# Three modulation banks of layer 1: out of the latent scan, into the loops of the first split FFN

## The chip, the core and the metric

The kernel runs on one core of one Trainium2 chip. The core has five engines that run at the same time, each through its own list of instructions and strictly in that list's order: TensorE (PE: matmuls, with its weight loads shown apart as PEld), VectorE (DVE), ScalarE (ACT), GpSimd (POOL) and SyncE (SP). They wait for one another through semaphores. SP, ACT and POOL also issue DMAs, which 16 DMA engines carry out; an issue that has to wait (for a buffer to come free) holds up whatever stands behind it in the same engine's list. The metric is the device time of one execution, in microseconds (us).

## What is computed

Two layers of a trunk over 128 context tokens and 1024 latent tokens, with 1024 features. Cut to what matters:

```python
def ada_mod(cond, w, b):
    m = (jax.nn.silu(cond) @ w + b)[..., None, :]
    return jnp.split(m, 6, axis=-1)

for i in range(DEPTH):                      # DEPTH = 2
    sh1c, sc1c, g1c, sh2c, sc2c, g2c = ada_mod(c_ctx, ada_w[i], ada_b[i])
    sh1l, sc1l, g1l, sh2l, sc2l, g2l = ada_mod(c, ada_w[i], ada_b[i])
    hc = modulate(xc, sh1c, sc1c)
    hl = modulate(xl, sh1l, sc1l)
    # layer 0: oc, ol = s5_mixer(hc), s5_mixer(hl): scan, output, gelu, GLU;  layer 1: pool_mixer
    xc = layer_norm(DEEPNORM_ALPHA * xc + g1c * oc, ln_g[i, 0], ln_b[i, 0])
    xl = layer_norm(DEEPNORM_ALPHA * xl + g1l * ol, ln_g[i, 0], ln_b[i, 0])
    fc = swiglu(modulate(xc, sh2c, sc2c), ffn_w_gate[i], ffn_w_up[i], ffn_w_down[i])
    fl = swiglu(modulate(xl, sh2l, sc2l), ffn_w_gate[i], ffn_w_up[i], ffn_w_down[i])
    xc = layer_norm(DEEPNORM_ALPHA * xc + g2c * fc, ln_g[i, 1], ln_b[i, 1])
    xl = layer_norm(DEEPNORM_ALPHA * xl + g2l * fl, ln_g[i, 1], ln_b[i, 1])
```

The modulation `ada_mod` depends only on the two conditioning vectors and on `ada_w` (1024 x 6144 in each layer), so it can be computed at any time before its first use. The first use of layer 1's modulation lies behind all of layer 0.

## The kernel before

The 1024 latent tokens are two blocks, A and B, of 512 tokens; the 128 context tokens are a third, C. A block lies feature-major: 128 partitions x 8 feature tiles x tokens. The latent GEMMs are *split* (lines 760 to 761 and 776 to 778): ACT writes a weight's high part `wh`, DVE the remainder `wl`, and PE makes three matmuls for each product. The context's GEMMs use the raw weight in one matmul (line 780), which the trace shows as two records. Weights come in blocks of 512 KB, by SP, into a ring of three buffers (`self.raw`, line 769); the splits have rings of three for `wh` and `wl`.

The modulation is cut into five banks of 2048 columns besides the first one: (layer 0: 1, 2; layer 1: 0, 1, 2). A bank is 16 steps of a generator (`ada_steps`, line 131). A step loads 512 KB of `ada_w` by SP (line 146, the tile `adaw`) and makes four matmuls of 32 x 256 on four column groups of the array (line 148), eight records in the trace. The 16th step goes on: ACT copies the sums out (`arow`, line 154), four small DMAs on ACT's queue regroup them (`ar`, line 158), PE transposes them (`adat`, line 160), and DVE adds the bias and derives vectors (line 161 and `vecs`). A caller takes steps with `self.step(fill, n)`, or one behind each item of a loop with `self.drain(loop, fill)`.

The program around the change runs in this order. `ssm` builds the states' inputs with 16 steps in its loops, then the context's mixer outputs (`ssm_y_ctx`) with another 16. Then come `ctx0a` (the context's GLU and LayerNorm), `ssm_scan_lat` (the latents' scan, on DVE) and the 48 steps of the three banks of layer 1; then `ssm_y` for eight feature tiles (matmuls `py`, lines 607 and 611; their gelu goes to DRAM as `yd`). While the pool `ssy` of this part is open, `self.adp` points to it and `adaw` has two buffers of its own there; once it is `None`, steps take their buffers, and `arow`'s, from `self.raw`, and their sums another PSUM tag. Behind `ssm`, `build` runs the context's channel mixing (`ctx0b`: 22 pairs of gate and up weights, then down weights; tile `rc`, from a pool in halves of a block, once the latents have theirs), reads the latents back (`yr`, line 1095, on POOL's queue, two buffers; `xr`, transposed by PE as `px`), then GLU of A and B, LayerNorm, and the split FFN of layer 0: `ffn_up` for A (22 pairs, 48 matmuls each), `ffn_down` for A (22 weights, 24 matmuls each), the same for B.

None of this fixes the order of the instructions alone. A scheduler takes the program's order as priority, simulates the engines, and writes each engine's list; so matmuls of `ctx0b`, the steps and `py` are interleaved on PE, and their loads on SP.

```python
self.ctx0a()
self.ssm_scan_lat()
self.step(fill, 48)
self.adp = self.rawc = None
for kt in range(KT):
    self.ssm_y(tmp, kt)
```

Of the kernel before, what the change touches and what calls it, by code (L numbers as in the profile page):

```python
# [11 lines left out]
F32 = mybir.dt.float32  # L12
# [5 lines left out]
DRAM = bass.MemoryType.DRAM  # L18
# [23 lines left out]
class Kernel:  # L42
# [3 lines left out]
    # ---------------------------------------------------------------- helpers  # L46
# [20 lines left out]
    def cmul(self, eng, pool, o_re, o_im, a, b, shape, tag, nb_im=None, p=None):  # L67
        """o = a * b for complex pairs; with nb_im = -b_im the imaginary part comes out negated."""
# [15 lines left out]
    # ------------------------------------------------------------- constants  # L84
    def consts(self):
# [16 lines left out]
        # mod[l]: [128, vec, cond, kt]; vec = sh1, sc1, g1, sh2, sc2, g2  # L102
# [27 lines left out]
    # --------------------------------------------------------- conditioning  # L130
    def ada_steps(self, l, b, pool=None):
        """Columns 2048*b.. of layer l's modulation, for both conditions, in small steps."""
# [45 lines left out]
    # ------------------------------------------------------------------ SSM  # L178
    def ssm_params(self, pool, tmp, ad):
# [31 lines left out]
        self.h0 = self.sk.tile([128, 2, 2, 32], F32, name="h0")   # dir, re/im, gpair  # L211
# [19 lines left out]
        # powers of the discretized diagonal: [128, re/im, exponent 0..8, (dir, gpair)]  # L231
# [12 lines left out]
        # input coefficient  # L244
# [15 lines left out]
        # scan multipliers per direction: [128, dir, (Rr|Rr|-?), ...]  # L260
        rm = self.sk.tile([128, 2, 2, 2, 32], F32, name="rm")      # dir, term, re/im, gpair
# [7 lines left out]
        # B and C with the states on the partitions: [128, re/im, (dir, gpair), 16]  # L269
# [28 lines left out]
    def ssm_modvec(self, pool, tmp, arow):  # L298
        """(1 + sc1) and sh1 per (token in chunk, channel) partition: [128, cond, (sh, sc), g]."""
# [20 lines left out]
    def ssm_u(self, tmp, kt):  # L320
        """u[(s,h), g, chunk]: the modulated mixer input; also the context's residual."""
# [23 lines left out]
    def ssm_u_ctx(self, tmp):  # L345
# [3 lines left out]
        # partitions are (feature tile, chunk)  # L349
# [25 lines left out]
    def load_x(self):  # L375
        """Feature-major residual of the latents."""
# [13 lines left out]
    def ssm_in(self, tmp, d, kt, tp, nb):  # L390
        """Chunk inputs V of direction d's state recurrence for 8 groups, written into the state slots."""
# [41 lines left out]
    def scan_step(self, *steps):  # L433
        """State slots: dst += A^8 src, for each (direction, src, dst); the steps are independent."""
# [37 lines left out]
    def ssm_dskip(self, pool, tmp):  # L472
        """D on the partitions (group of 8, h'): [128, kt]; selector of h == h'; zeroed B blocks."""
# [12 lines left out]
        # block-diagonal B of group pairs: [128 = (group of 2, state), dir, re/im, pair, (group of 2, h')]  # L486
# [4 lines left out]
    def ssm_tables(self, tmp, kt, si):  # L491
        """Output tables and in-chunk kernels of 8 groups, to DRAM in the layout of the output products."""
# [59 lines left out]
    def ssm_y_ctx(self, tmp, kt):  # L552
        """Mixer output (after gelu) of the context for 8 groups, feature-major."""
# [29 lines left out]
        # the last ones stay on chip: partitions (group pair, chunk); a group's features go to its own columns,  # L583
        # the rest of them stay zero
# [12 lines left out]
    def ssm_y(self, tmp, kt):  # L597
        """Mixer output (after gelu) of the latents for 8 groups, to DRAM feature-major."""
# [23 lines left out]
    def ssm(self):  # L622
# [43 lines left out]
        with R("ssy") as tmp:  # L666
# [11 lines left out]
            self.step(fill, 48)  # L678
# [13 lines left out]
    def ctx0a(self):  # L692
        """The context's mixer output projection of layer 0."""
        C, xmc = self.C, self.xmc
        self.glu(C, [xmc], vx=lambda a: a.rearrange("p (c t) -> p t c", t=8),
                 vs=lambda a: a.rearrange("p (t c) -> p t c", t=8))
        self.ln(C, 0, 0, [xmc])

    def ctx0b(self):
        """The context's channel mixing of layer 0, in steps."""  # L700
# [5 lines left out]
    def ctx1a(self, tmp):  # L706
        """The context's pool mixer."""
# [8 lines left out]
    def ctx1b(self):  # L716
        """The context's channel mixing of layer 1, in steps."""
# [6 lines left out]
    # -------------------------------------------------------- derived vectors  # L724
# [498 lines left out]
```

## Time and profile before

| | before |
|---|---|
| runs (3), median | 2500.75 us |
| lowest, highest | 2499.89, 2501.96 us |
| span of the profiled execution | 2493.0 us |
| median less that span | 7.75 us |
| PE busy in the span | 2296.9 us (92%) |
| DMA moved in the span | 370.63 MB, 149 GB/s |
| steps (`adaw` loads, 512 KB each) | 96, of which 48 are issued from 307.21 us on |

The profiled execution has no device time of its own in the records, only its span. Times below are us from the span's start. "PEclk" is the clock that was granted to TensorE, as a share of the full one; the DMA share is the mean busy share of the 16 DMA engines. A stretch in which PE has gaps and the DMA share is about 1 waits for data; one in which PE is busy throughout is bound by PE.

### The profile page before, as it was taken

How to read it: one execution, taken by the hardware profiler on the slowest of the kernel's cores; microseconds unless marked ns; L12 is line 12 of the kernel's file. 1: busy time of each engine (PE TensorE's matmuls, PEld its weight loads, DVE VectorE, ACT ScalarE, POOL GpSimd, SP SyncE). 2: the span in 40 equal slices, each digit the busy share in tenths (PEclk: the TensorE clock that was granted, in tenths of full speed). 3: DMA queues.
4: the chain of work that ended last, by engine and by line, in shares of the span. 5: the costliest groups of instructions: out<-in, count | busy, mean ns of one | idle time of the engine just before them, and what ended most of it. 6: DMA issues, size and time to landing. Idle time of an engine off the chain costs nothing.

```text
span 2493.0 us, 33897 instructions
## 1 busy us (share of the span) xinstructions
PE 2296.9 (92%) x13533; PEld 1880.8 (75%) x13533; DVE 1252.8 (50%) x2429; ACT 895.0 (36%) x1321; POOL 191.2 (8%) x190
## 2 busy tenths in 40 slices
PE   4685779979999999999999999889999999999997
PEld 2453557668888788888888888777788888888996
DVE  7579771024444632455422585778422455422476
ACT  3673211134423422433422353325322443322464
POOL 4760000000001000100000010002000100000000
PEclk8897889999999999999999999999999999999998
DMA  7767888796454333223333224874333223333352
GB/s 219 218 203 286 278 262 262 219 313 178 142 156 129 101 93 100 95 98 96 94 98 97 99 96 137 236 204 142 94 96 97 95 93 95 92 97 96 136 202 103
DMA packets 465246, 370.63 MB, mean 149 GB/s; under 512 B 19792, under 2 KB 414816, under 8 KB 462784
## 3 DMA queue, kind: packets, MB, share of 16 engines
q1 hardware_dynamic: 445296, 349.29, 45.5%
q10 hardware_dynamic: 18448, 14.58, 1.8%
q0 software_dynamic: 1344, 4.59, 0.5%
q8 instruction: 106, 1.74, 0.3%
q14 instruction: 52, 0.43, 0.1%
HBM read 345.36 MB, written 22.94 MB: 148 GB/s over the span
## 4 chain that ended last, share of the span: by engine, by line
PE 79%; DMA 13%; ACT 3%; DVE 2%; SPq 1%; issue 1%; POOL 1%; ACTq 0%; DVEq 0%; POOLq 0%
PE ffn L778 13%; PE ffn L776 13%; PE ffn L777 13%; PE dn L777 6%; PE dn L776 6%; PE dn L778 6%; PE ffn L780 4%; DMA adaw<-ada_w 3%; PE py L611 3%; PE dn L780 2%; DMA raw<-ffn_w_up 2%; PE glu L777 2%; PE glu L778 2%; PE glu L776 2%; DMA raw<-ffn_w_gate 2%; PE ada L148 1%
## 5 line engine op out<-in xcount | busy, mean ns | idle before, releaser
L760 ACT ACTIVATE wh<-raw 128x1024 fp32r<-128x1024 f32 (+1 forms) x326 | 341.6, 1049 | 944.0 <-PE ffn L777 619.6
L761 DVE TENSOR_TENSOR wl<-raw,wh 128x1024 fp32r<-128x1024 f32 (+1 forms) x326 | 394.6, 1211 | 482.9 <-ACT wh L760 475.5
L777 PE MATMUL dn<-hkl,wh 128*128 128x512 f32 (+1 forms) x880 | 304.3, 348 | 0.3 <-DVE hkl L761 0.3
L778 PE MATMUL dn<-hkh,wl 128*128 128x512 f32 (+1 forms) x880 | 302.9, 347 | 0.0
L776 PE MATMUL ffn<-xp,wh 128*128 128x512 f32 x704 | 280.3, 398 | 2.3 <-ACT wh L760 2.3
L778 PE MATMUL ffn<-xp,wl 128*128 128x512 f32 x704 | 280.5, 398 | 0.5 <-DVE wl L761 0.5
L777 PE MATMUL ffn<-xp,wh 128*128 128x512 f32 x704 | 278.1, 395 | 0.0
L776 PE MATMUL ffn<-xm,wh 128*128 128x512 f32 x704 | 273.3, 390 | 2.8 <-ACT wh L760 2.1
L778 PE MATMUL ffn<-xm,wl 128*128 128x512 f32 x704 | 275.7, 392 | 0.0
L777 PE MATMUL ffn<-xm,wh 128*128 128x512 f32 x704 | 274.9, 390 | 0.2 <-DVE xm L761 0.2
L776 PE MATMUL dn<-hkh,wh 128*128 128x512 f32 (+1 forms) x880 | 259.4, 347 | 0.8 <-ACT hkh L760 0.8
L821 DVE TENSOR_TENSOR h<-ffn,sg 128x512 f32<-128x512 f32 x88 | 60.5, 688 | 254.0 <-PE ffn L778 253.3
L777 PEld LDWEIGHTS dn<-hkl,wh 128*128 128x128 f32 x880 | 166.6, 189 | 21.1 <-DVE hkl L761 0.5
L778 PEld LDWEIGHTS dn<-hkh,wl 128*128 128x128 f32 x880 | 166.5, 189 | 20.5
L776 PEld LDWEIGHTS dn<-hkh,wh 128*128 128x128 f32 x880 | 163.3, 189 | 21.8 <-ACT hkh L760 1.3
L780 PE MATMUL ffn<-xmc,raw 128*128 128x128 f32 x1184 | 150.1, 284 | 23.4 <-DMA raw<-ffn_w_gate 10.6
L780 PEld LDWEIGHTS ffn<-xmc,raw 128*128 128x128 f32 x1184 | 142.3, 197 | 37.7 <-DMA raw<-ffn_w_up 13.9
L776 PEld LDWEIGHTS ffn<-xp,wh 128*128 128x128 f32 x704 | 132.7, 189 | 34.1 <-ACT wh L760 2.5
L777 PEld LDWEIGHTS ffn<-xp,wh 128*128 128x128 f32 x704 | 132.9, 189 | 33.8 <-issue 0.7
L778 PEld LDWEIGHTS ffn<-xp,wl 128*128 128x128 f32 x704 | 132.9, 189 | 33.8 <-DVE wl L761 1.0
L776 PEld LDWEIGHTS ffn<-xm,wh 128*128 128x128 f32 x704 | 132.5, 188 | 32.2 <-ACT wh L760 3.0
L777 PEld LDWEIGHTS ffn<-xm,wh 128*128 128x128 f32 x704 | 132.5, 188 | 28.4 <-DVE xm L761 0.9
(305 smaller groups left out, 3209.5 us busy)
## 6 DMA issues: line engine op xcount, KB each, us to landing
raw<-ffn_w_down SPq DMA_DIRECT2D x126, 512.0 KB
raw<-ffn_w_gate SPq DMA_DIRECT2D x125, 512.0 KB
raw<-ffn_w_up SPq DMA_DIRECT2D x125, 512.0 KB
adaw<-ada_w SPq DMA_DIRECT2D x96, 512.0 KB
raw<-ssm_glu_w SPq DMA_DIRECT2D x48, 512.0 KB
mo<-mo SPq DMA_DIRECT2D x16, 1536.0 KB
rc<-ffn_w_down SPq DMA_DIRECT2D x40, 256.0 KB
mo<-otab SPq DMA_DIRECT2D x16, 512.0 KB
```

Source lines behind the costliest of these rows:

```text
L148: nc.tensor.matmul(ps[32 * cg:32 * cg + 32, 256 * hf:256 * hf + 256], self.cond[:, k, :], w[:, cg * 256:(cg + 1) * 256], start=(k == 0), s ...
L611: nc.tensor.matmul(o[x], ot[64 * x:64 * x + 64, d, r, gp, :], self.Z[d][64 * x:64 * x + 64, d:d + NCL, 32 * r + 4 * kt + gp], start=False, ...
L760: nc.scalar.activation(h, src, AF.Copy)
L761: nc.vector.tensor_tensor(l, src, h.bitcast(F32), op=OP.subtract)
L776: nc.tensor.matmul(ps, wh, xh, start=start, stop=False)
L777: nc.tensor.matmul(ps, wh, xl, start=False, stop=False)
L778: nc.tensor.matmul(ps, wl, xh, start=False, stop=stop)
L780: nc.tensor.matmul(ps, w[0], x[0], start=start, stop=stop)
L821: nc.vector.tensor_tensor(h[:, f, :], pu, sg, op=OP.mult)
```

## The change

The call that takes the 48 steps behind the scan is gone. Nothing is put in its place: the generator is still held as `self.ada`, and the loops of layer 0's split FFN already draw from it (`fill = self.ada`, then `drain` of `ffn_up(A)`, `ffn_down(A)` and `ffn_up(B)`, each with `fill`). Before, it was empty there. Now it gives one step behind each of A's 22 pairs, one behind each of A's 22 down weights, and the last four behind B's first pairs. Since `self.adp` is `None` by then, their loads and `arow` take buffers of `self.raw`.

```diff
             self.ctx0a()
             self.ssm_scan_lat()
-            self.step(fill, 48)
             self.adp = self.rawc = None
             for kt in range(KT):
                 self.ssm_y(tmp, kt)
```

The rest of the diff takes out comments and docstrings. Lines behind 678 have one number less in the changed kernel (780 becomes 779).

PE's list from the context's LayerNorm (`lnm`, `lnv`) to the latents' output products, before (`ffn` is the context's channel mixing, `ada` a step):

```order
L148 MATMUL ada_3997<-adaw_4046,cond 32x256 x4
L780 MATMUL ffn<-xmc,raw 128x128 x8
L148 MATMUL ada_3997<-adaw_4052,cond 32x256 x4
L780 MATMUL ffn<-xmc,raw 128x128 x5
L148 MATMUL ada_3997<-adaw_4058,cond 32x256 x4
L780 MATMUL ffn<-xmc,raw 128x128 x11
L148 MATMUL ada_3997<-adaw_4064,cond 32x256 x4
L148 MATMUL ada_3997<-adaw_4070,cond 32x256 x4
L780 MATMUL ffn<-xmc,raw 128x128 x24
```

and now:

```order
L779 MATMUL glu<-xmc,raw 128x128 x37
L862 MATMUL lnm<-lt,ones 128x128
L862 MATMUL lnv<-sq,ones 128x128
L779 MATMUL ffn<-xmc,raw 128x128 x100
L611 MATMUL py_4000<-Z_648,mo 128x128
...
L779 MATMUL ffn<-xmc,raw 128x128 x44
L611 MATMUL py_4000<-Z_1796,mo 128x128
```

The steps are gone from between the context's matmuls. Eight matmuls are one weight: 144 of them, 18 weights, now stand ahead of the main run of `py`, where 14 weights stood; 12 instead of 16 stand behind it. On SP the `adaw` loads between the weights' loads are gone likewise.

PE's list in `ffn_up` of block A, at the end of the 16th pair (`ffn_7905` is its up product, `ffn_7969` the next gate product), before:

```order
L776 MATMUL ffn_7905<-xm_5092,wh 128x512
L777 MATMUL ffn_7905<-xm_5093,wh 128x512
L778 MATMUL ffn_7905<-xm_5092,wl 128x512
L776 MATMUL ffn_7969<-xm_5092,wh 128x512 [waits Activation_49]
L777 MATMUL ffn_7969<-xm_5093,wh 128x512
```

and now, where the first of the three banks ends (`adaw_7728` is its 16th load, `ffn_7745` and `ffn_7746` the next pair):

```order
L777 MATMUL ffn_7664<-xm_4760,wl 128x512
L148 MATMUL ada_6662<-adaw_7728,cond 32x256 [waits DMAHW0_49]
L148 MATMUL ada_6662<-adaw_7728,cond 32x256 x3
L160 MATMUL adat_7741<-ident,ar_7736 128x32 [waits DMAHW5_49,DMAHW6_49,DMAHW4_49,DMAHW3_49]
L775 MATMUL ffn_7745<-xm_4760,wh 128x512 [waits Activation_49]
L776 MATMUL ffn_7745<-xm_4761,wh 128x512
L775 MATMUL ffn_7746<-xm_4760,wh 128x512 [waits Activation_49]
```

A step stands behind each pair, and the bank's transpose directly behind its 16th step, with no matmul between. The second bank ends in the same way in `ffn_down` of A, the third behind the fourth pair of B.

ACT's list at the same place now (`sg` is the pair's gate, the four DMAs wait for `arow`):

```order
L819 ACTIVATE sg<-ffn_7663 128x512 [waits DVE_49,PE_49]
L154 ACTIVATE arow_7734<-ada_6662 128x512 [waits DMAHW2_49,DVE_49,PE_49]
L158 DMA ar_7736<-arow_7734 8x1x128 [waits Activation_49]
L158 DMA ar_7736<-arow_7734 8x1x128
L158 DMA ar_7736<-arow_7734 8x1x128 [waits DMAHW5_49]
L158 DMA ar_7736<-arow_7734 8x1x128
L759 ACTIVATE wh<-raw 128x1024 [waits DMAHW1_49]
L759 ACTIVATE wh<-raw 128x1024 [waits DMAHW2_49]
```

The copy and its four DMAs stand ahead of the next pair's two splits.

## Rows read from the trace of the kernel before

**Rows 1.** The page: busy tenths of PE and the DMA engines in 40 slices.
```profile
PE   4685779979999999999999999889999999999997
DMA  7767888796454333223333224874333223333352
```

**Rows 2.** Windows: stretch, length, busy of PE, PEld, DVE, ACT, POOL; PEclk, DMA, GB/s.
```profile
298.00:329.00 31.00, 25.34 (x227) 20.89 (x227) 26.50 (x156) 2.80 (x7) 0.00 (x0) 1.00 0.99 299
...
389.00:484.50 95.50, 95.50 (x756) 68.20 (x754) 0.83 (x4) 9.95 (x18) 0.00 (x0) 1.00 0.70 230
484.50:524.00 39.50, 32.84 (x305) 27.27 (x304) 1.75 (x6) 3.67 (x9) 0.00 (x0) 1.00 1.04 304
524.00:564.20 40.20, 29.24 (x195) 23.62 (x196) 14.07 (x20) 21.44 (x32) 3.25 (x6) 0.96 0.98 313
...
600.00:665.50 65.50, 65.50 (x336) 55.90 (x335) 22.46 (x25) 22.53 (x25) 0.00 (x0) 1.00 0.45 130
...
1064.00:1180.00 116.00, 116.00 (x512) 95.67 (x511) 63.20 (x73) 46.23 (x62) 0.00 (x0) 1.00 0.28 91
```

**Rows 3.** The chain that ended last, from 340 to 490: start, length, what.
```profile
343.85 3.71 PE ffn L780 x16
...
386.74 2.05 PE ffn L780 x16
...
404.24 0.64 PE py L607 x4
404.88 1.93 PE py L611 x16
...
421.81 1.48 PE py L611 x10
...
423.86 1.04 PE py L611 x6
...
486.50 0.57 PE ada L148 x8
487.07 1.09 PE ffn L780 x8
```

**Rows 4.** Timeline of SP's queue: start, length, queue, line, operation, tile, count.
```profile
329.98 21.00 SPq L146 DMA_DIRECT2D adaw<-ada_w  x8
```

**Rows 5.** Timeline of POOL, from 330 to 620 (idle before, and its releaser, in brackets).
```profile
340.83 5.72 POOL L914 TENSOR_SCALAR xmc<-XC,lnm 128x128 f32<-128x128 f32 x8 [66.09 <-issue]
536.14 1.13 POOL L1095 DMA_DIRECT2D yr<-yd  x2 [189.59 <-ACT X L387]
```

**Rows 6.** SP's queue in the context FFN of layer 1: first and last of 25 issues.
```profile
1529.27 0.37 SPq L769 DMA_DIRECT2D raw<-ffn_w_up  x1
...
1583.79 0.37 SPq L769 DMA_DIRECT2D raw<-ffn_w_up  x1
```

**Rows 7.** SP's queue behind the latents' outputs.
```profile
520.41 1.85 SPq L146 DMA_DIRECT2D adaw<-ada_w  x2
...
535.64 0.93 SPq L1189 DMA_DIRECT2D rc<-ffn_w_gate  x2
```

**Rows 8.** Timeline at the end of the first bank, where nothing else stands on PE.
```profile
47.47 1.08 PE L148 MATMUL ada<-adaw,cond 128*32 128x256 f32 x8 [0.32 <-DMA adaw<-ada_w]
...
49.24 2.97 ACTq L158 DMA_DIRECT2D ar<-arow  x4
...
53.59 0.28 PE L160 MATMUL adat<-ident,ar 32*128 32x32 f32 x1 [5.04 <-DMA ar<-arow]
```

**Rows 9.** Timeline of PE behind a short idle time in the split FFN.
```profile
816.00 0.50 PE L776 MATMUL ffn<-xm,wh 128*128 128x512 f32 x1 [2.12 <-ACT wh L760]
...
819.64 0.50 PE L776 MATMUL ffn<-xm,wh 128*128 128x512 f32 x1
```

**Rows 10.** The page's groups of the two splits: busy us, mean ns of one, idle before.
```profile
L760 ACT ACTIVATE wh<-raw 128x1024 fp32r<-128x1024 f32 (+1 forms) x326 | 341.6, 1049 | 944.0 <-PE ffn L777 619.6
L761 DVE TENSOR_TENSOR wl<-raw,wh 128x1024 fp32r<-128x1024 f32 (+1 forms) x326 | 394.6, 1211 | 482.9 <-ACT wh L760 475.5
```

## The prediction

> **What bounds the kernel now.** First the page [rows 1]: PE is at nine tenths in most slices, and its low digits lie in the first eight slices, just where the DMA digits are 6 to 9; from about the eleventh slice on PE is full and the DMA engines a third busy. So the kernel has two regimes, data first and PE later, and the change moves 48 steps from the first to the second. Then the windows [rows 2], to see where between 298 us and 665 us which of the two holds. In the context's GLU (298 to 329) the DMA engines are at 0.99 and PE has gaps. While the latents' outputs `py` are made (389 to 484.5) PE is busy for all of 95.50 us and the DMA engines have room (0.70). From 484.5 to 564.2 it is data again: 304 and 313 GB/s, DMA share about 1, PE idle for 17.6 of 79.7 us. From then on PE has the work: the share falls to 0.45 by 600 to 665.5, with PE full, and to 0.28 in the FFN of layer 0 (1064 to 1180), where 512 matmuls take 116.00 us, 0.227 each. The chain [rows 3] gives the prices on PE in these stretches, SP's and POOL's lists [rows 4 to 7] what the loads wait for, and three places outside of them [rows 8 to 10] what a bank's end, a short idle time and a weight's split cost. So a step that goes is worth its DMA time in two stretches and its PE time in a third, and a step that comes costs its PE time in a stretch where PE has none to spare.
>
> **What is gained: the outputs start earlier.** Of the 48 loads, the first of them issued at 307.21, three stand ahead of the last GLU weights; at 0.524 MB and 299 GB/s they are 5.3 us of DMA time. With them gone the ring of three buffers sets the pace: alone it brings 24 weights in 54.5 us, 2.27 us each [rows 6]. I take 4 us of the 5.3. Then the LayerNorm, where PE waits in any case, and the first weight, which POOL's `xmc` paces (5.72 us from 340.83 [rows 5]): it ended at 343.85 + 3.71 = 347.56 [rows 3], with steps standing ahead of it on PE; without them and 4 us earlier it ends soon after the last `xmc`, at about 342. Then 17 weights more, since 18 instead of 14 now stand ahead of `py`: two lie in the ring, one at the lower clock (3.71) and one at the full one (2.05), then 15 x 2.27 = 34.1; together 39.8, so `py` begins at about 382. Before, it began at 386.74 + 2.05 = 388.8, though with four weights less, because SP stood for 21 us with eight step loads ahead of the next weight [rows 4]. Ends: 378.5 if PE (2.05 each) paces, 388.8 if nothing is won.
>
> **The outputs get shorter.** Twenty records of `py` take 0.64 + 1.93 = 2.57 us where nothing cuts in [rows 3]; 640 are 82.2 us, and ten of them (1.5) stand earlier, so 80.8 remain of 95.7. The 18 steps in between took 18 x 0.57 = 10.3; the rest, 4.6, is what a cut costs: the sixteen records of 1.93 us took 1.48 + 1.04 with a step in them. So `py` ends at 382 + 80.8 = 463 instead of 484.5, which is 21.5 us.
>
> **The stretch behind them has less to move.** Before: 39.5 x 304 + 40.2 x 313 = 24.6 MB [rows 2]. Ten step loads fall away (the last two at 520.41 [rows 7]), 5.2 MB, and the four weights that now stand ahead, 2.1 MB. 17.3 MB at 308 GB/s are 56 us. `yr` and the first `rc` loads waited for the pool `ssy`, which the last bank held until 535.64 [rows 5, 7]; now the last `yd` write holds it, a few us behind `py`, and until then only the ring loads (231 GB/s by its 2.27): 2 us more. 58 instead of 79.7, to 521 instead of 564.2. Behind it PE is full as before, so it all counts: **43 us gained**. Ends: 33, if `py` begins where it did (388.8 + 80.8 = 469.6) and the stretch takes 62; 51, if `py` begins at 378.5 and the stretch takes 54.
>
> **What is paid: 48 steps where PE is full.** A step is 0.57 us, and the eight records behind one took 1.09 where half of 2.05 is 1.03 [rows 3]: 0.63, x 48 = 30.4. I take this row and not the cut in `py` (0.6 more), since `py` runs in pairs on half of the rows and the FFN's matmuls use all 128, as these do. The loads are 0.524 MB for every 6 or 11 us in a stretch whose DMA share is 0.28 [rows 2]; they hide there. Ends: 27.4 and 33.
>
> **Three ends of a bank.** PE's list has the transpose directly behind the 16th step, so PE stands through the copy and four DMAs: 5.04 us, and 0.28 for itself [rows 8]; x 3 = 16.0. Before, the three transposes lay behind other work. Queued behind the waiting one are all of the FFN's matmuls; behind the four issues (2.97 us of ACT's queue) stand the next two splits, 1.05 each with 1.21 on DVE [rows 10]. Counted from the step, the first `wl` comes at about 0.6 + 3 + 1.05 + 1.2 = 5.9 and the second `wh` at 5.8, where PE asks at 5.3 to 6: nothing to a further 1 us each; I take nothing and keep 3 for the range.
>
> **The clock behind each.** After 2.12 us of idle time PE needed 3.64 us for nine starts [rows 9], which the full clock gives in 9 x 0.227 = 2.04 [rows 2]: 1.6 lost; x 3 = 4.8. After the longer idle time ahead of 343.85 one weight lost 1.66 [rows 3], so 2.5 each is the upper end.
>
> The sum of the costs is 30.4 + 16.0 + 4.8 = **51 us**, between 46 (steps at 0.57, two of them in the gaps of B's LayerNorm, the clock half as dear) and 60 (33, 19, 7.5).
>
> Net 51 - 43 = +8. On the profiled span, 2493.0 + 8 = 2501; the runs' median is 7.75 above that span, so **2509 us**.
>
> **The rivals.** *The gain is smaller.* The ring alone might not keep its pace beside `mo` and `xr`, and `py` begin at 388.8; then 33 are gained, +18, 2519 us. For it: the loads of the GLU took longer than 2.27 with the DMA engines full. Against it: no step load stands between them any more.
>
> *Faster: the ends of the banks don't stall and the gain is full.* If the four DMAs of `ar` land while PE still works off queued matmuls, only the steps are paid, 30.4, and at a gain of 43 it comes out at -13: 2488 us. It decides at the place of the transpose: four or five matmuls, 5.3 us of them, between the 16th step and the transpose would do. Against it: the list has none.
>
> *Faster by regimes.* If every step load had lengthened a stretch bound by data, 48 x 0.524 = 25.2 MB at 308 GB/s, 82 us, would be gained, and 51 - 82 = -31: 2470 us. Against it: 18 of the steps ran beside `py`, where PE and not data was the bound [rows 2], and eight in the LayerNorm. The Trainium skill, in "Perfetto Trace Analysis" (Optimization Strategy), says that a kernel whose most contended engine changes over time may gain by interleaving its regimes, which is this change's shape; by that rule alone one would expect this rival's sign. The windows agree that there are two regimes, but the rule leaves out that a step brings PE work with its bytes.
>
> *Slower still: the FFN's ring starves.* A step's load takes a buffer out of three in `self.raw`. In `ffn_down` a step and a weight alternate every 24 x 0.227 + 0.6 = 6.0 us. If the down weights have one buffer, each must land and be split before the next is asked for: by the ring's cycle of 3 x 2.27 less one weight on PE (2.05), 4.8, plus 1.05 + 1.21 = 7.0. Then each of 22 weights loses up to 1.0, and +8 becomes +30: 2531 us. It decides where landing takes more than 3.7 us. Against it: these loads have a third of the DMA's share beside them, and the splits run ahead by up to three.
>
> *Nothing to be measured.* Gain and cost are both near 50 and cancel within 5 us: 2496 to 2506. About 0.2%, 5 us, is what a measurement of this kernel can tell from no change.
>
> **How the numbers follow.** The forecast (+2 to +16) has 0.50, and about a third of that lies within 5 us; the smaller gain 0.20; the ends without a stall 0.11; regimes 0.04; the starving ring 0.06; the exact cancelling 0.09. Faster: 0.11 + 0.04 = 0.15. Within 0.2%: 0.16 + 0.09 = 0.25. Slower: the rest, 0.60. The range leaves out both faster rivals' times and the starving ring's, some 0.2: from 2495 (cost 46, gain 51, so -5 or 2496, and 1 us of scatter) to 2524 (cost 58 with a gain of 35).
>
> **What would show it.** Right, step by step: the main run of `py` begins near 382 and holds no `ada`; it ends near 463; a stretch of some 58 us at 300 GB/s follows, and the first down product of the context (665.5 before) comes some 43 us earlier. Then 48 groups `ada` of about 0.57 us in A's FFN and the first pairs of B; three idle times of about 5 us on PE released by the DMA `ar`, each with a lower PEclk for some us behind it. PE's waits for `wh` or for `raw` weights there should not grow. Wrong: `py` that begins at 388 (smaller gain); no 5 us of idle time at the transposes (faster); waits of PE for `wh` at each down weight (the ring); a first down product later than 640.

## The result and the profile of the changed kernel

The changed kernel took 2522.0 us (median of 4 runs, 2520.2 to 2526.8) against 2500.3 for the kernel before on the same chip; the ratio is 1.0099, 95% interval [1.0083, 1.0114]. It is slower by 21.7 us. The forecast was 2509, so +8: the sign was right and the time lies inside the range, near its upper end, but of the 21.7 us of loss it had only 8. The two profiled executions differ by 2518.4 - 2493.0 = 25.4 us, and the working below is made on those. (The changed kernel's profiled run took 2520.19, 1.8 us over its span; of the kernel before, the run of 2494.85 fits its span in the same way. The "7.75" of the prediction set the median against the span of what was probably the fastest run, which shifts both kernels and not the difference.)

| us from the span's start | before | changed | difference | foreseen |
|---|---|---|---|---|
| first context FFN matmul | 343.85 | 344.29 | +0.4 | about -4 |
| `xmc` starts (POOL, end of the context's LayerNorm) | 340.83 | 342.44 | +1.6 | -4 |
| last step of the scan on DVE ends | 383.35 | 387.81 | +4.5 | not named |
| main run of `py` starts | 388.7 | 390.8 | +2.1 | 382 |
| `py` ends | 484.5 | 469.7 | -14.8 | 463 |
| first split FFN product of block A | 793.89 | 760.79 | -33.1 | -43 |
| sums of block B's second LayerNorm start | 1431.63 | 1456.82 | +25.2 | +8 |
| end | 2493.0 | 2518.4 | +25.4 | +8 |

So the part in front gained 33 instead of 43, and the split FFN paid 58 instead of 51: +25. The windows of the changed kernel, by stretch (length, busy time and count of PE, PEld, DVE, ACT and POOL, granted clock, DMA share, GB/s), answer to [rows 2]:

```profile
298.00:331.00 33.00, 27.06 (x231) 23.39 (x229) 27.54 (x163) 3.14 (x8) 0.00 (x0) 1.00 0.84 252
331.00:344.30 13.30, 1.24 (x5) 0.81 (x5) 13.24 (x63) 3.26 (x8) 1.86 (x2) 0.67 0.18 50
344.30:391.00 46.70, 40.80 (x310) 38.10 (x312) 32.43 (x176) 7.51 (x18) 4.06 (x7) 0.95 0.65 185
391.00:469.70 78.70, 78.70 (x611) 63.15 (x610) 0.29 (x1) 9.14 (x17) 0.00 (x0) 1.00 0.52 159
469.70:531.00 61.30, 45.03 (x354) 41.65 (x354) 19.91 (x26) 30.27 (x46) 4.29 (x8) 0.97 0.98 301
```

The loads did leave: the GLU's stretch falls to a DMA share of 0.84, the LayerNorm's to 0.18 and that of `py` to 0.52. In the LayerNorm's 13.3 us nothing takes the steps' place: PE is busy for 1.24 us of them while DVE is busy throughout. Behind `py` stand 61.3 us at 301 GB/s, 18.4 MB; that stretch is as full of data as before and only shorter.

In the split FFN two places tell where the time is paid. First PE at an ordinary step (start, length, line, tiles; the length of one matmul overlaps the next, so the distance of starts is what counts):

```profile
823.07 0.39 PE L777 MATMUL ffn<-xm,wl 128*128 128x512 f32 x1
823.39 0.64 PE L148 MATMUL ada<-adaw,cond 128*32 128x256 f32 x8
823.96 0.50 PE L775 MATMUL ffn<-xm,wh 128*128 128x512 f32 x1
824.30 0.39 PE L776 MATMUL ffn<-xm,wh 128*128 128x512 f32 x1
...
835.07 0.64 PE L148 MATMUL ada<-adaw,cond 128*32 128x256 f32 x8
```

From one step to the next are 835.07 - 823.39 = 11.68 us; the 48 products between them need 48 x 0.2266 = 10.88. A step costs 0.80: 0.57 from its start to the next product's, 0.09 because the product ahead gives it 0.32 instead of 0.227, and 0.11 because the first product behind gives the second 0.34.

Then PE's waits between 760 and 1450 (what waited for what, total, times, longest), and the place of the first bank's end on PE (with the window behind it), ACT, DVE and SP (idle time before an instruction, and its releaser, in brackets), which answers to [rows 8]:

```profile
PE adat L160 <- DMA ar<-arow: 13.0, 3, 4.5
PE ffn L777 <- DVE wl L760: 1.5, 1, 1.5
PE ffn L775 <- ACT xm L759: 0.7, 1, 0.7
```

```profile
951.87 0.64 PE L148 MATMUL ada<-adaw,cond 128*32 128x256 f32 x8
956.96 0.28 PE L160 MATMUL adat<-ident,ar 32*128 32x32 f32 x1 [4.45 <-DMA ar<-arow]
957.17 0.80 PE L775 MATMUL ffn<-xm,wh 128*128 128x512 f32 x1
957.77 0.63 PE L776 MATMUL ffn<-xm,wh 128*128 128x512 f32 x1
958.20 0.63 PE L775 MATMUL ffn<-xm,wh 128*128 128x512 f32 x1
```

```profile
957.17:959.50 2.33, 2.33 (x7) 1.84 (x7) 1.98 (x4) 0.67 (x2) 0.00 (x0) 0.50 0.53 160
```

```profile
952.58 0.60 ACT L154 ACTIVATE arow<-ada 128x512 f32<-128x512 f32 x1 [5.44 <-PE ada L148]
953.21 2.27 ACTq L158 DMA_DIRECT2D ar<-arow  x4
955.52 2.00 ACT L759 ACTIVATE wh<-raw 128x1024 fp32r<-128x1024 f32 x2 [2.35 <-DMA ar<-arow]
```

```profile
956.61 1.23 DVE L760 TENSOR_TENSOR wl<-raw,wh 128x1024 fp32r<-128x1024 f32 x1 [3.87 <-ACT wh L759]
```

```profile
940.89 0.37 SPq L768 DMA_DIRECT2D raw<-ffn_w_gate  x1
952.57 0.37 SPq L768 DMA_DIRECT2D raw<-ffn_w_up  x1
956.96 0.34 SPq L146 DMA_DIRECT2D adaw<-ada_w  x1
957.86 0.37 SPq L768 DMA_DIRECT2D raw<-ffn_w_gate  x1
```

PE stands for 4.45 us, then works at the lower clock for five starts (0.43 apart instead of 0.227; the granted clock of that window is 0.50). To the next step, at 969.70, are 17.83 us instead of 11.68: 6.15 for one bank's end, taken three times below (the third costs 6.25, the second, where a piece of another step follows the transpose, about 5.6). The ACT rows show the copy and its DMAs ahead of the next two splits, and the SP rows show the up weight of the next pair issued at 952.57, directly behind the 16th step: until then a step's load had held its buffer. (An ordinary pair has its up weight issued 11.6 us ahead of its first product, 824.09 for 835.64; here it is 4.6 us.) Two bounds end here nearly together: the transpose starts at 956.96, and the first split of the next pair, held behind `arow` and its DMAs though its weight was issued at 940.89, is done at about 956.6, when DVE goes on from it. So by these rows moving the transpose alone would win back some 0.4 us. What `arow`'s place in the ring has to do with it is what two experiments below are for.

### The profile page after: what moved, and what is told of

It reads as the page before. It is cut to its first block, busy times and chain, and to the rows that moved or that the text cites. A ratio compares the mean times of both kernels' runs of the same rounds, so it can differ in the third digit from the quotient of the medians.

```text
span 2518.4 us, 33876 instructions
## 1 busy us (share of the span) xinstructions
PE 2308.6 (92%) x13533; PEld 1880.2 (75%) x13533; DVE 1252.2 (50%) x2429; ACT 894.5 (36%) x1321; POOL 185.3 (7%) x190
## 4 chain that ended last, share of the span: by engine, by line
PE 78%; DMA 10%; issue 4%; DVE 3%; ACT 2%; POOL 1%; SPq 1%; ACTq 0%; POOLq 0%; DVEq 0%
PE ffn L775 13%; PE ffn L777 13%; PE ffn L776 13%; PE dn L775 6%; PE dn L776 6%; PE dn L777 6%; PE ffn L779 3%; PE py L611 2%; PE dn L779 2%; PE glu L777 2%; PE glu L775 2%; PE glu L776 2%; DMA adaw<-ada_w 2%; PE ada L148 2%; DMA raw<-ffn_w_gate 1%
## 5 line engine op out<-in xcount | busy, mean ns | idle before, releaser
L775 PE MATMUL dn<-hkh,wh 128*128 128x512 f32 (+1 forms) x880 | 273.3, 351 | 0.9 <-ACT hkh L759 0.9
L775 PEld LDWEIGHTS ffn<-xm,wh 128*128 128x128 f32 x704 | 132.9, 189 | 37.9 <-issue 9.4
L777 PEld LDWEIGHTS ffn<-xm,wl 128*128 128x128 f32 x704 | 132.7, 189 | 30.6 <-DVE wl L760 2.0
```

The source lines that it names most:

```text
L775: nc.tensor.matmul(ps, wh, xh, start=start, stop=False)
L777: nc.tensor.matmul(ps, wl, xh, start=False, stop=stop)
```

## The experiments

The kernel before ran beside every one of them (2497.97 to 2498.39 in these jobs, against 2500.3 beside the changed kernel), so differences of up to about 2 us between jobs mean nothing; those within a job are better. Stretches of the profiles help where PE is full; a profile's front scatters by 6 us (below), and the part from block B's second LayerNorm sums to the end, which no edit touches, lasts from 1060.9 to 1068.8 us.

**The 48 steps left out.** This kernel leaves out the modulation of layer 1 (a constant stands in its place), so its time is what the removal alone is worth.

```diff
-                fill = self.ada
+                fill = iter(())
+                for i in range(3):
+                    nc.vector.memset(self.mod[1][:, 2 * i:2 * i + 2], 0.5)
+                    self.vecs(1, i)
```

> The changed kernel with the 48 steps left out altogether: the three banks of layer 1 hold a constant, so what layer 1 computes is not the reference's. It shows what the removal is worth without what the new places cost. If the first stretch gains what the trace of the changed kernel shows (33 us), the time is about 2500 - 33 = 2467 us; by the sum of the prediction, 43 us, it would be 2457; if every one of the loads had lengthened a stretch that waits for data, 82 us, 2418.

It took 2460.7 us, ratio 0.9855 [0.9836, 0.9874]. That lies between the two figures of the expectation, 2467 and 2457. So the removal gains 37 us and no more, and the regimes' rival, which made it 82, falls. Its `py` starts at 388.4 and ends at 467.2: the start did not move, although no step is anywhere. Against it the changed kernel pays 2522.0 - 2460.7 = 61.

**The loads alone.** The kernel before with the steps' matmuls at the same place in the program, but reading an array that is in SBUF anyway (`self.adfix`, 1024 columns of `u`), without their loads (so the modulation of layer 1 is not that of the reference).

```diff
-                w = ring(1024, f"adaw{l}{b}{k}{hf}")
                 c0 = b * 2048 + hf * 1024
-                nc.sync.dma_start(w, I["ada_w"][l, k * 128:(k + 1) * 128, c0:c0 + 1024])
+                if l:
+                    w = self.adfix
+                else:
+                    w = ring(1024, f"adaw{l}{b}{k}{hf}")
+                    nc.sync.dma_start(w, I["ada_w"][l, k * 128:(k + 1) * 128, c0:c0 + 1024])
```

> The kernel before with the matmuls of the 48 steps where they were, but without their loads: they read a tile that lies in the chip already, so the three banks hold other numbers than the reference's. Theory 1, the loads are what the steps cost there, and only where data is awaited: the ten loads behind the latents' outputs are worth 5.2 MB at 308 GB/s, 17 us, and the others up to 5, so some 2480 us, with the outputs still ending late (within 4 us of before). Theory 2, the loads held up SP's queue and so the scan's stretch too: 30 us or more, 2470 or less.

2475.4 us, ratio 0.991 [0.9891, 0.993]: 22.6 us less, between the two theories' times, and the condition of the first is broken: the outputs end at 458.50, 26 us earlier than before. The matmuls did not stay where they were on PE:

```profile
341.21 9.38 PE L151 MATMUL ada<-u,cond 128*32 128x256 f32 x128 [1.07 <-DVE mod L164]
...
360.64 7.11 PE L151 MATMUL ada<-u,cond 128*32 128x256 f32 x128
...
379.71 1.12 PE L614 MATMUL py<-Z,mo 64*128 64x128 f32 x8
```

With no load to wait for, the scheduler put all 48 steps ahead of the main run of `py`, 32 of them in these two rows, and nine weights there instead of 14. So the run starts at 379.71, and it lasts 78.8 us, as long as in the kernel without steps. The 22.6 us are the worth of the loads and of this other order together, and the 14.7 that remain of the 37 are not the price of the 18 steps inside `py`: in this kernel none stands there. (What those cost is read from the runs of `py`, 95.8 us before and 78.9 in the changed kernel.) The second row gives the price of a step among its like: 16 in 7.11 us, 0.44 each.

**A ring of its own for the steps.** The changed kernel, with two buffers for the steps' loads and for `arow` beside the FFN's ring, and the PSUM tag that the steps used in the scan.

```diff
+                adf = tc.tile_pool(name="adf", bufs=1)
+                self.adp = adf.__enter__()
                 fill = self.ada
...
                 self.drain(fill)
+                adf.__exit__(None, None, None)
+                self.adp = None
```

> The changed kernel, but the 48 steps in the FFN have a ring of two buffers of their own for their loads and for the row that is copied out, so that they take none of the weights' three. In its list the bank's transpose stands 41, 162 and 41 matmuls behind the 16th step, not directly behind it. Theory 1, the ends of the banks cost some 6.2 us each (idle time and lower clock): three idle times of 4.1 to 4.5 us go, PE runs on, and the time falls by 15 to 19 us from 2522, to about 2505. Theory 2, the price lies in the steps alone and the idle time would come back elsewhere, since the splits stand behind the four DMAs on ACT: it falls by less than 5 us.

2497.2 us, ratio 1.0001 [0.9989, 1.0013]: the loss is gone, 24.9 us of it with this one edit, which is more than the 15 to 19 expected. No wait of PE for `adat` is left.

**A buffer for `arow` alone.** To split those 25: the steps' loads stay in the shared ring, only the row that ends a bank leaves it.

```diff
-                else ring(512, f"arow{l}{b}"))
+                else ring(512, f"arow{l}{b}") if l == 0 else
+                self.arp.tile([128, 512], F32, tag="arow", name=f"arow{l}{b}", bufs=1))
...
+                adf = tc.tile_pool(name="adf", bufs=1)
+                self.arp = adf.__enter__()
```

> The change with one thing altered: the row that ends a bank (arow) has a buffer of its own, the 48 weights of the steps still share the ring raw with the FFN. Theory (three bank ends cost 6.2 us each because arow waits for a buffer of raw and the FFN's next weight splits stand behind it on ACT; the rest of what the shared ring costs is the steps that were cut in two): 2522 minus 18 = 2502 to 2506. Rival (it is the weights of the steps in the ring that cost, not arow): 2517 to 2522. Rival (arow is all of it): 2497, as with a ring for all.

2502.4 us, ratio 1.0023 [1.0013, 1.0033]: 19.6 of the 24.9. The rows of this kernel at the first bank's end, PE and then ACT:

```profile
948.55 0.64 PE L148 MATMUL ada<-adaw,cond 128*32 128x256 f32 x8
...
958.65 0.24 PE L161 MATMUL adat<-ident,ar 32*128 32x32 f32 x1
...
960.65 0.64 PE L148 MATMUL ada<-adaw,cond 128*32 128x256 f32 x8
```

```profile
949.26 1.06 ACT L760 ACTIVATE wh<-raw 128x1024 fp32r<-128x1024 f32 x1 [4.72 <-PE ada L148]
950.22 0.58 ACT L155 ACTIVATE arow<-ada 128x512 f32<-128x512 f32 x1
```

A split now stands ahead of `arow` on ACT, the transpose stands nine us of FFN products behind the 16th step instead of directly behind it, and it waits for nothing; no wait for `adat` is left on PE. The expectation's wording was wrong in one point: in the changed kernel it is not `arow` that waits (it starts 0.07 us after the step). So `arow` in the ring makes the stall, and it makes it by the order: with `arow` there, the next pair's up weight comes late and both its splits are put behind `arow`, so that the transpose has nothing to hide behind. Why the scheduler also put the gate's split there, whose weight was in time, is not shown.

**The steps in pairs, by fours, and by fours close together.** All with the ring of their own (four buffers for the fours). The generator that hands them out, here for the fours; the last kernel has one `yield None` in place of the loop of three.

```diff
-                fill = self.ada
+                fill = self.twos(self.ada)
...
+    def twos(steps):
+        while True:
+            for _ in range(3):
+                yield None
+            for _ in range(4):
+                if next(steps, 0) == 0:
+                    return
+            yield None
```

> As the kernel with the ring of its own, but the steps come two at a time, behind every second pair or weight: 24 places instead of 48, the same loads and matmuls. Theory 1, a place costs PE about 0.23 us of switching beside its matmuls, whatever stands in it (0.80 us a step, and 1.0 + 0.23 for two, by the changed kernel's trace): 8 to 10 us less than with single steps. Theory 2, the price is that of the matmuls: no more than 2 us of difference.

> The change with its own ring of four buffers in the FFN, and the steps handed out four at a time. Theory (a step costs by the place at which it cuts the FFN's matmuls: about 0.80 us for a place of up to 8 records, 1.23 for 16): the order has 22 places there instead of 32 with pairs, 7 of 16 records, 3 of 11 to 13, 12 small ones: 7x1.23 + 3x1.1 + 12x0.8 = 21.5 us, against some 25.5 for the pairs as ordered; so about 2490 to 2491, from the pairs' 2494.6. Rival (a step costs by its records, whatever the place): no change, 2494.6. Rival (four loads that are asked for at one time make PE wait for them): slower, with waits of ada for adaw.

> As the kernel with fours, but the groups of four follow each other after every second instead of every fourth pair of tiles, so that all three banks lie in the first split FFN's upper half and none is cut up in the down loop: the order has 10 places of four steps behind the LayerNorm and a few steps ahead of it. Theory (the records of the fours give 0.57 us to the next start for one step, 1.00 for two, 1.86 for four, and some 0.22 around each place: 0.43 per step and 0.36 per place): 48x0.43 + 11x0.36 = 24.6 over the kernel without steps (2460.7), so 2484 to 2488; by the same sum the kernel with fours, 26 places, is at 2490.7 and had 2491.0. Rival (the price is per step alone, and the fours gained by something else): 2491. Rival (four loads every 23 us, closer together than before, make PE or the weights' ring wait): over 2491, with waits for adaw or wh.

Measured: pairs 2494.6 (ratio 0.9982 [0.9969, 0.9994]), fours 2491.0 (0.9968 [0.9958, 0.9977]), fours close together 2489.5 (0.997 [0.9957, 0.9983]). Two and four steps on PE, of the pairs' kernel and of the last one, each with the product ahead and the first two behind:

```profile
851.76 0.39 PE L777 MATMUL ffn<-xm,wl 128*128 128x512 f32 x1
852.08 1.07 PE L148 MATMUL ada<-adaw,cond 128*32 128x256 f32 x16
853.08 0.51 PE L775 MATMUL ffn<-xm,wh 128*128 128x512 f32 x1
853.42 0.40 PE L776 MATMUL ffn<-xm,wh 128*128 128x512 f32 x1
```

```profile
831.83 0.39 PE L777 MATMUL ffn<-xm,wl 128*128 128x512 f32 x1
832.15 1.93 PE L148 MATMUL ada<-adaw,cond 128*32 128x256 f32 x32
834.02 0.50 PE L775 MATMUL ffn<-xm,wh 128*128 128x512 f32 x1
834.35 0.40 PE L776 MATMUL ffn<-xm,wh 128*128 128x512 f32 x1
```

The pairs' theories both missed: 2.6 us less than the own ring with single steps, by the medians, where 8 to 10 or at most 2 were expected. The order held 32 places, not 24, and the single steps 47, not 48. The fours came out at the 2491 that was expected, but that is no evidence for the theory: their median is 3.6 us below that of the pairs, while the FFN's stretch, where the theory acts, is only 0.5 shorter (table).

From the first step's start to the next product are 0.57, 1.00 and 1.87 us for 8, 16 and 32 records: 0.43 per step, and 0.14 once per place; with the 0.09 ahead and some 0.11 to 0.13 behind a place costs 0.36 besides its steps. (The expectation of the fours took the 16 matmuls of four steps for 16 records and priced them at 1.23 instead of about 2.1, and the pairs too low by the same slip, so that the difference of the two came out near what was measured all the same.) The formula against the stretch from block A's first FFN product to the sums of B's second LayerNorm, where PE is full; without steps that stretch takes 636.1 us:

| kernel | places | stretch, us | over 636.1 | 48 x 0.43 + places x 0.36 |
|---|---|---|---|---|
| changed | 53 | 696.0 | 59.9 | 39.7, and 18.4 for three bank ends: 58.1 |
| `arow` alone | 50 | 676.7 | 40.6 | 38.6 |
| own ring | 47 | 673.1 | 37.0 | 37.6 |
| pairs | 32 | 668.2 | 32.0 | 32.2 |
| fours | 26 | 667.7 | 31.6 | 30.0 |
| fours close together | 15 | 665.7 | 29.6 | 26.0 |

The measured excess differs from the sum by -0.6 to +3.6 us, and the traces show most of the reasons. The three transposes of 32 x 32, places too, cost 0.39 each where they stand between products, though there is next to nothing in them; that is the price of a place once more. PE's waits are 2.2, 0.9, 1.0, 1.4 and 3.4 us in the last five rows, against 3.0 in the kernel without steps. A step cut into pieces costs more than its share of 0.43: a piece of two records takes PE as long as one of eight, so the rows with pieces (`changed`, `arow` alone, fours) come out low. And in the last kernel a wait of 1.8 us at 1094 is followed by eight starts at the lower clock (granted 0.64 from 1094.5 to 1098.8), 1.6 us more.

The last kernel missed its expectation (2484 to 2488), and its rival, waits from loads too close together, has a part in it: 3.4 us of waits for `hkh`, `hkl` and `adaw`, and that clock. By its ratio to the kernel before (0.9970) it can't be told from the fours (0.9968), both 0.3% ahead of the kernel before.

**One bank left in the scan, the others by fours.**

```diff
             self.ssm_scan_lat()
+            self.step(fill, 16)
             self.adp = self.rawc = None
```

> As the kernel with fours, but one of the three banks (16 steps) stays in the scan and its bank end lies there too. Theory (in the place between the context's LayerNorm and its FFN, 13.3 us with PE busy for 1.24 and the DMA engines at 0.18, about eight loads and their matmuls are free; the other eight cost the mean of the scan, 0.78 each): it costs 6 us and saves a third of the 21.5 us in the FFN, 7 us: 2487 to 2491. Rival (all 16 cost the scan's mean, 37.3/48 each): 12.4 us for 7, 2496.

2492.9 us, ratio 0.9979 [0.9969, 0.9988]: the theory's 2487 to 2491 was missed, and so was the rival's 2496. The 16 steps put block A's first FFN product from 759.59 to 772.95, 13.4 us later (the rival's 12.4), and shorten the FFN by 667.7 - 656.2 = 11.5. So a step in the scan costs about 0.84 with its load; the medians, 1.9 us above the fours in the same job, agree with 13.4 - 11.5, but the two profiles' fronts differ by 5.5 us at `xmc` already, so the 0.84 is rough. That the LayerNorm's stretch, with PE and the DMA engines idle, is a free place for eight of them isn't borne out; why not is open.

**Fewer context steps between the outputs and the GLU.**

```diff
-            self.step(fill, 15)
+            self.step(fill, 11)
```

> The change with 11 instead of 15 steps of the context's FFN handed out ahead of the latents' blocks: the order ahead of the scan's outputs is the same, behind them 7 weights fewer (56 matmuls) stand between the outputs and the GLU. Theory (the 61 us behind the outputs are set by the bytes, 18.4 MB at 300 GB/s, so fewer bytes there end it earlier, and the weights moved find room in the GLU where the DMA share is below a half): the GLU is full 8 to 12 us earlier, 2510 to 2514. Rival (the stretch is set by the chain of yr loads and the splits on ACT and DVE, 6 us a load, eight of them): 2520 to 2524.

2530.6 us, ratio 1.0131 [1.0116, 1.0145]. Both theories missed the time, but the stretch behind `py` settles its question:

```profile
470.10:509.70 39.60, 24.92 (x203) 22.57 (x201) 13.45 (x16) 24.68 (x37) 3.76 (x7) 0.97 1.02 324
```

39.6 us at 324 GB/s, 12.8 MB, where the changed kernel has 61.3 us and 18.4 MB. The eight `yr` loads are issued over 35 us there (475.45 to 510.28) and over 32 in the changed kernel (474.87 to 507.32), so they do not need 61 us; the bytes set this stretch in the changed kernel, and the chain of `yr` falls as its bound. (With the shorter stretch it may be the next one: the last load is issued as the stretch ends.) But what was won there was lost again, and more: the context's FFN now runs on to 792.8 instead of 754.07, into the split FFN, whose stretch (to the same LayerNorm sums) lasts 722.5 us instead of 696.0.

**Why the outputs start no earlier: the scan's waits.** The scan on DVE in the changed kernel (start, length, line, tiles; idle time before, and its releaser, in brackets):

```profile
379.41 0.23 DVE L443 TENSOR_TENSOR Z<-stt,Z 128x64 f32<-128x64 f32 x1
382.06 0.29 DVE L820 TENSOR_TENSOR hc<-ffn,sg 128x128 f32<-128x128 f32 x1 [2.42 <-ACT sg L819]
382.26 0.22 DVE L443 TENSOR_TENSOR Z<-stt,Z 128x64 f32<-128x64 f32 x1
...
387.33 0.48 DVE L443 TENSOR_TENSOR Z<-stt,Z 128x64 f32<-128x64 f32 x2
391.22 0.29 DVE L820 TENSOR_TENSOR hc<-ffn,sg 128x128 f32<-128x128 f32 x1 [3.40 <-ACT sg L819]
```

The scan's steps (L443) stand in one list with the context's gated products `hc`. Each `hc` waits for `sg`, that for a matmul, that for a weight, and the scan's next step waits behind it. The scan ends at 387.81, and `py` starts 3.0 us later. The theory made of it was that these waits hold the start. The experiment takes nine of the products off DVE:

```diff
-            nc.vector.tensor_tensor(h[:, f, :], pu, sg, op=OP.mult)
+            if l == 0 and not b.split and f < 9:
+                nc.scalar.activation(h[:, f, :], pu, AF.Copy)
+                nc.gpsimd.tensor_tensor(h[:, f, :], h[:, f, :], sg, op=OP.mult)
+            else:
+                nc.vector.tensor_tensor(h[:, f, :], pu, sg, op=OP.mult)
```

> The change with the gated products hc of the first nine tiles of the context's FFN on GpSimd (ScalarE copies one factor out of PSUM) instead of VectorE; the order on PE ahead of the scan's outputs stays, 18 weights. Theory (the latents' scan runs on VectorE and stands behind these products, each of which waits for a weight that is still loading: 13.3 us in nine waits, so that the scan's last step ends at 387.8 and the outputs cannot start before): the scan ends by 378, PE no longer waits for hc (6.0 us in six) and the run of outputs starts at 383 to 386 instead of 390.8; 2515 to 2518. Rival (the 18 weights ahead on PE hold the start by their loads alone): the scan ends earlier but the start stays at 389 to 391 and the time at 2520 to 2524.

> Both together, the steps by fours in the upper half and the context's first nine gated products on GpSimd. Theory (the two act in different stretches and add up): the time of the one less what the other gave, about 2480 if the products give 5 to 7, 2486 if they give nothing. Rival (what the products give is given back in the data-bound stretch behind the outputs): 2486.

Of the first kernel, POOL at the end of the context's LayerNorm, DVE at the end of the scan, and PE around the start of the main run:

```profile
337.62 5.92 POOL L917 TENSOR_SCALAR xmc<-XC,lnm 128x128 f32<-128x128 f32 x8 [57.08 <-issue]
```

```profile
372.03 0.49 DVE L443 TENSOR_TENSOR Z<-stt,Z 128x64 f32<-128x64 f32 x2
```

```profile
378.08 2.05 PE L779 MATMUL ffn<-xmc,raw 128*128 128x128 f32 x16 [0.38 <-DMA raw<-ffn_w_up]
380.72 4.00 PE L779 MATMUL ffn<-xmc,raw 128*128 128x128 f32 x30 [0.58 <-ACT hc L821]
384.64 1.12 PE L611 MATMUL py<-Z,mo 64*128 64x128 f32 x8
```

At first sight the theory holds: the scan ends at 372.5 and `py` starts at 384.64 instead of 390.80, 6.2 us earlier. But the time is 2523.7 us (1.0097 [1.0076, 1.0119]) against 2522.0, and both together 2490.5 (0.9969 [0.9957, 0.9982]) against 2489.5 for the fours alone; no gain is measured (the intervals are some 3 to 5 us either way). What the first sight missed is that the part of the run in front of the context's FFN scatters from one profile to the next. In the changed kernel `xmc` starts at 342.44, here at 337.62, for work that the edit doesn't touch. Counted from `xmc`:

| kernel | `xmc` starts | scan ends | `py` starts | `py` less `xmc` |
|---|---|---|---|---|
| before (14 weights ahead) | 340.83 | 383.35 | 388.72 | 47.9 |
| changed | 342.44 | 387.81 | 390.80 | 48.4 |
| steps left out | 340.31 | 385.68 | 388.39 | 48.1 |
| loads alone left out (nine weights ahead) | 342.75 | 376.19 | 379.71 | 37.0 |
| own ring | 337.54 | 385.84 | 388.42 | 50.9 |
| `arow` alone | 337.84 | 383.24 | 385.92 | 48.1 |
| pairs | 339.62 | 385.27 | 388.26 | 48.6 |
| fours | 338.99 | 385.08 | 387.80 | 48.8 |
| fours close together | 339.18 | 385.36 | 388.56 | 49.4 |
| one bank left in the scan | 344.50 | 389.79 | 393.77 | 49.3 |
| fewer context steps | 343.33 | 388.57 | 391.38 | 48.1 |
| `hc` off DVE | 337.62 | 372.52 | 384.64 | 47.0 |
| both together | 337.76 | 372.66 | 385.00 | 47.2 |

Counted from `xmc`, the scan ends 10 to 13 us earlier and the start comes only 1 to 4 us earlier, most often 1 to 2. So the rival is right for the most part: the 18 weights ahead, which end right behind the scan's waits, hold the start. It spoke of their loads alone, but most of it is their time on PE, which is busy for 40.80 of the 46.70 us between the first weight and `py` in the changed kernel. Its waits there (what waited for what, total, times, longest):

```profile
PE ffn L779 <- DMA raw<-ffn_w_up: 3.4, 4, 2.0
PE ffn L779 <- DMA raw<-ffn_w_gate: 1.6, 3, 0.6
PE ffn L779 <- DVE hc L820: 0.7, 1, 0.7
```

That is 5.0 us for weights and 0.7 for `hc`, where the expectation had 6.0 in six for `hc`. The scan's waits that were read were real, and were not worth what they showed. (Of the "13.3 us in nine waits" 3.4 also lie behind the scan's end; 9.9 lie in it, against 9.2 in the kernel before.)

## Why the prediction was partly right

**What held.** The sign and its two columns: a gain in front that is worth less than the price in the FFN. The run of `py` is 78.9 us long instead of 95.8 (80.8 foreseen; 610 records stand in it, where the sum had 630) and ends 14.8 us earlier, though it starts 2.1 later. The ends of the banks stall as worked out: 4.1 to 4.5 us of idle time each and a lower clock behind, 6.15 us in all against 5.3 + 1.6 = 6.9 in the sum. The splits behind `arow`, which the sum had worked out to end at about the same time and took for nothing, did so. The FFN's ring did not starve otherwise: besides those for `adat`, PE's waits there are 2.2 us in two, against 3.0 without any step. The two faster rivals fell, the one because the transposes do stand bare, the other because the removal is worth 37 us and not 82. (The former asked for "four or five matmuls, 5.3 us of them" ahead of the transpose; at 0.227 us each, 5.3 us are 23.)

**The rival that came nearest.** *The gain is smaller* had `py` beginning at 388.8, 33 us gained and 2519 us, at a chance of 0.20. Measured were 390.8, 33.1 us and 2522.0. Its reason, the ring's pace, holds only in small part: the last fifteen weights ahead of `py` took 2.38 us each instead of 2.27.

**Step "the outputs start earlier": failed, 9 us missing in the gain.** Two of its terms. The GLU was to end 4 us earlier, which puts the start of `xmc` at 336.8; it was 342.44 in this profile, and 339.9 in the mean of the eight kernels that have this front (337.5 to 343.3), so the loads that left were worth about 1 us there, less than the scatter. And from `xmc` to `py` 45.2 us were allowed; it took 48.4, and 48.1 to 50.9 in the others with 18 weights ahead and `hc` on DVE. Counted from `xmc`, the first three weights took 9.8 us instead of 10.9, the fifteen behind them 35.7 instead of 34.1, and 2.9 are twenty records of `py` that stand between the weights (as they did in the kernel before): the sum took ten of them off the run, and left out that they take their time ahead of it. On PE of the changed kernel they are one row:

```profile
375.97 2.87 PE L611 MATMUL py<-Z,mo 64*128 64x128 f32 x20
```

The scan's end was not looked at: it came at 383.35 before, behind its waits for `hc`, so with these waits 382 was out of reach. They were not the only bound: with the scan ending at 372.5 the start is 384.64. In the one kernel with only nine weights ahead, and no loads of steps beside them, it is 379.71.

**Step "the stretch behind them": mis-sized by 3.** 18.4 MB at 301 GB/s, 61.3 us, instead of 17.3 MB at 308 and 2 us more. The bound was the right one: with 5.6 MB less it is 39.6 us.

**Step "48 steps where PE is full": mis-sized by 8.** 0.63 was taken from [rows 3], where the step cuts into 128 x 128 matmuls of the context, and the cut in `py` (0.6 more, [rows 3]) was put aside. In the split FFN the price was 0.80, of which 0.36 belongs to the place and 0.43 to the step: 48 x 0.17 = 8. The Trainium skill, in "TensorEngine Tiling (Array Packing)" (Key Properties), says that changing the tiling mode drains TensorE; a step works on 128 x 32 tiles, the FFN on 128 x 128, so each place has two such changes. The rows agree with the sentence, at 0.36 us for the two changes of a place, and 0.39 for a transpose of 32 x 32; that the price goes by places is shown by the kernels with fewer of them. That it is the drain, and not something else that changes with the tile, no run here separates. The prediction did not weigh that rule.

**Not foreseen: steps cut up.** In A's down loop the scheduler spread some steps over several places, 53 places in all for 48 steps: 5 x 0.36 = 1.8 us by the sum. That is a lower bound: at 0.78 to 0.80 us for every place of two to eight records and 1.2 for the two larger ones, the 53 places cost 43, where 48 whole steps would cost 38.4.

The balance by steps: gain 33.1 instead of 43 (-10: the start -8.8, the run +1.9, the stretch -3.3); cost 48 x 0.43 + 53 x 0.36 = 39.7 instead of 30.4, bank ends 18.4 instead of 20.8, sum 58.1 (58.3 measured against the kernel before) instead of 51 (+7). 8 + 10 + 7 = 25. Part of the 10 is no step's fault: two profiles differ by up to 6 us in the front, and the removal is worth 37 by medians. And the sum of 58.1 comes out near the measured 58.3 with two small things left out, the pieces' full price on one side and, on the other, waits and a lower clock that the kernel before has in this stretch and the changed one has not.

## What to carry to other kernels

A filler that uses another tile shape than the loop it is put into is paid for per place, so it should come in groups, each with all its data there; here the same 48 steps cost 60 us one by one with a shared ring and 30 in fours with their own. Before work is handed from one ring to another, look at what else takes buffers from that ring, and which instruction is left without cover when the next weight comes late. And before a difference of a few us between two profiles is put down to an edit, count it from a point that the edit touches, and look at how that point itself scatters.

## What had not been expected

- Two, four, six or eight records of a step all take 0.55 to 0.57 us to the next FFN product, ten, 12 or 16 take 0.98 to 1.00, and 32 take 1.87: cutting a step into pieces doubles its price or worse.
- The same instructions in the same order reach the end of the context's LayerNorm between 337.5 and 343.3 us in eight profiles, though the median of the kernel before repeats to 0.1% from job to job.
- Without their loads the steps moved to other places on PE, so that an edit meant to take away the loads alone changed the order as well.
- Taking 20 us out of the stretch behind the outputs made the whole slower by 8.6 us, because PE work of the context that had been free there landed in a stretch where PE is full.
